# Where the chunked scan stands in the order of emission: each group's scan behind the next group's projections

## The chip, the cores and the metric

The kernel runs on one core of a Trainium2 chip. The metric is the device time of one execution in microseconds (us). Each time is the median of several executions; the profile is of one execution of the same program. The engines are TensorE (PE, matmuls), VectorE (DVE), ScalarE (ACT), GpSimd (POOL) and SyncE (SP), which issues most DMAs.

## The reference, cut to what matters

One layer of a hybrid backbone over 512 latent tokens and 256 context tokens, in float32. One input projection feeds three branches: a bidirectional chunked scan (SSD), a pooling mixer and a gated branch (gMLP). They are merged, projected and followed by a mixture of experts. The part in question:

```python
xbc = silu(dwconv(cols[..., :XBC_W], conv_w, conv_b))      # x, B, C of 4 groups, 5 taps
dt = softplus(cols[..., XBC_W:] + dt_bias)
# per direction, per group, chunks of 128:
acum = cumsum(dt * a)
decay = exp(where(tri, acum_i - acum_j, -inf))
y_diag = (C B^T * decay) @ (x * dt)
states = B^T @ (x * dt * exp(acum_last - acum))             # then a scan over the chunks
y_off = (C @ h_in) * exp(acum)
y = y_diag + y_off, both directions added; y_ssd = rmsnorm((y + d_skip * x) * silu(z))
# gated branch
u, v = gelu(uv); v = layernorm(v); y_gmlp = u * (ws @ v + bs)
# pooling branch: box means of width 2, 4, 8, 16 over the 8 x 64 grid, minus the input, then a matmul
```

## The kernel before

Every float32 weight comes by a DMA of 512 KB into a `raw` buffer (four), is split into a high part on ACT (L87, `hi`, three buffers) and a low part (L89, `lo`, three buffers), and goes into three matmuls: high by high, high by low, low by high. In the stage of the change POOL computes the low part (`lo_eng` is G).

Projections take one of three forms. `xbc_tile` (L997) projects 128 channels of x, B or C over 512 tokens (24 matmuls of 512 columns) and, but for C, over 256 context tokens (24 of 256), and hands the result to `conv_tile` (L951): copies on ACT into `xr` (two buffers), a first tap on ACT (L967), four taps on DVE (L969), silu on ACT, six transposes on PE (L989, L991) and copies to token order on ACT (L992, L993). `tm_block` (L1134) projects 512 columns in token order with 96 matmuls into all four accumulator banks (`pacc`); `z_block` (L1164) and `v_block` (L1210) use it. `cm_block` (L1148) projects 256 channels with 48 matmuls into two banks; pooling, `u_block` and the gates use it.

The scan works on four groups of four heads. For each group g:
- `bc(g)` and `xx(g)`: B and C, then two tiles of x, by `xbc_tile`;
- `ssd_decay(g)` (L1107): for four chunks, C B^T on PE (L1115), masks on DVE, the decay from a row that is broadcast by DMA from DRAM (`agb`, two buffers, L1111), exponentials on ACT, all joined in `w` (L1124 to L1132). `w` has four buffers, one group's worth;
- `z_block` for even g: the silu-gated z of two groups, into `ytok`;
- `ssd_group(g)` (L1053): the scan. DVE weights x (`xe`, L1061 to L1063), then five steps for two directions: a state matmul (L1074) and two DVE operations (L1083, L1084); then for each chunk matmuls with the states (L1093) and with `w` (L1095), and five DVE operations (L1099 to L1103), the last of which multiplies into `ytok`.

BT, CT, btok and xtok have two buffers each, so two groups can be held at once. Three PSUM banks (`ptmp`) serve the transposes, the products of the decay and the scan.

Behind the four groups the gated and the pooling branch are emitted as: pooling block 1, `v_block`, pooling block 0, `pool_out(1)`, `u_block(0)`, `pool_out(0)`, `u_block(1)`. Pooling is mostly DVE additions (L1259 to L1279) on `hx`, a tile that takes the buffer of the context tokens' `hC`; its matmul is on L1285. `v_block` writes its normalised v into `hx` too, and `u_block` mixes it (L1231). Then come the norm of the scan's output (squares on L1309), the gates and the merge.

The order on the engines' queues is not the order of emission. A framework lays out each engine's queue when the program is built: it goes by its own estimate of durations, and of the instructions that it takes to be ready the one that was emitted first goes first. On the chip each queue runs strictly in the order laid out. The order in which the Python code calls the steps is therefore a precedence. Before the change it is:

```python
for g in range(4):
    bc(g); xx(g); ssd_decay(g)
    if g % 2 == 0: z_block(g // 2)
    ...                                # g == 0: mix_prep(), params2(), zero
    nc.sync.dma_start(...)             # zero fill of one part of eod, from tile zero
    ssd_group(g)
```

Of the kernel before, what the change touches and what calls it, by code (L numbers as in the profile page):

```python
# [7 lines left out]
FT = mybir.dt.float32  # L8
# [3 lines left out]
AF = mybir.ActivationFunctionType  # L12
OP = mybir.AluOpType
# [16 lines left out]
OFF_GMLP = 3616  # L30
OFF_GATE = 4640
PW = 7712
# [6 lines left out]
def dap(t, off, ap):  # L39
    return bass.AP(tensor=t.tensor, offset=t.offset + off, ap=ap)  # L40
# [3 lines left out]
def backbone_kernel(ctx: ExitStack, tc: tile.TileContext, x, c, ctxt, c_ctx, w_mod, b_mod, g_norm1,  # L44
# [3 lines left out]
    nc = tc.nc  # L48
    V, S, G, T = nc.vector, nc.scalar, nc.gpsimd, nc.tensor
# [11 lines left out]
    eod = drp.tile([L, D], FT)  # L61
# [6 lines left out]
    small = ctx.enter_context(pool("small", 2))  # L68
# [679 lines left out]
    hcp = ctx.enter_context(pool("hcp"))  # L748
# [131 lines left out]
    zero = ssd.tile([128, 128], FT)  # L880
# [226 lines left out]
    def ssd_decay(g):  # L1107
        for cc in range(4):
            t = 2 + cc
            agb = ep.tile([128, 2, 4, 128], FT, tag="agb", name="agb")  # L1110
            nc.sync.dma_start(agb.rearrange("p d k i -> p (d k i)"),  # L1111
                              dap(agd, (cc * 4 + g) * 1024, [[0, 128], [1, 1024]]))
            cs = slice(cc * 128, (cc + 1) * 128)
            pcb = ptmp([128, 128])
            T.matmul(pcb, lhsT=BT[g][:, cs], rhs=CT[g][:, cs], start=True, stop=True)  # L1115
            cbl = ep.tile([128, 128], FT, tag="cbl", name="cbl")
            cbu = ep.tile([128, 128], FT, tag="cbu", name="cbu")
            V.tensor_tensor(cbl, pcb, mge, op=OP.mult)
            V.tensor_tensor(cbu, pcb, mle, op=OP.mult)
            w = epw.tile([128, 4, 128], FT, tag="w", name="w")  # L1120
            e = agb[:, 0]
            for k in range(4):
                f, b = g * 4 + k, 16 + g * 4 + k
                S.activation(w[:, k], agb[:, 1, k], AF.Identity, bias=nag[:, t, b:b + 1])  # L1124
                V.scalar_tensor_tensor(e[:, k], agb[:, 0, k], ag[:, t, f:f + 1], w[:, k],  # L1125
                                       op0=OP.subtract, op1=OP.min)
            S.activation(e, e, AF.Exp)
            for k in range(4):
                f, b = g * 4 + k, 16 + g * 4 + k
                S.activation(w[:, k], cbu, AF.Copy, scale=dtt[:, t, b:b + 1])  # L1130
                V.scalar_tensor_tensor(w[:, k], cbl, dtt[:, t, f:f + 1], w[:, k], op0=OP.mult, op1=OP.add)  # L1131
            wts[g, cc] = w, V.tensor_tensor(w, w, e, op=OP.mult)  # L1132
# [36 lines left out]
    def bc(g):  # L1169
        xbc_tile(8 + g)  # L1170
        xbc_tile(12 + g)

    def xx(g):
        xbc_tile(2 * g)
        xbc_tile(2 * g + 1)

    for g in range(4):
        bc(g)
        lo_eng[0] = G
        xx(g)  # L1180
        ssd_decay(g)
        if g % 2 == 0:
            z_block(g // 2)
        if g == 0:
            mix_prep()
            params2()
            with tc.issue_after(wts[0, 3][1].ins):
                V.memset(zero, 0.0)
        nc.sync.dma_start(dap(eod, g * 1024, [[4096, 128], [128, 8], [1, 128]]),
                          zero[:, None, :].to_broadcast([128, 8, 128]))  # L1190
        ssd_group(g)
    lo_eng[0] = G
    sq_.close()

# [7 lines left out]

    with ExitStack() as p3:
        gp = p3.enter_context(pool("gp"))
        hx = hcp.tile([128, 4096], FT, tag="h", name="hx")
        vt = hx[:, 0:2048].rearrange("p (t n) -> p t n", t=4)
        xps = [hx[:, n:n + 640].rearrange("p (r q) -> p r q", r=8) for n in (2048, 2688)]
        m = hx[:, 3328:3840].rearrange("p (t n) -> p t n", t=4)

        def v_block():  # L1210
            pv = tm_block(w_in, PW, OFF_GMLP + 512)
            for t in range(4):
                v = vt[:, t]
                S.activation(v, pv[t], AF.Gelu_apprx_tanh)
                bn = small.tile([128, 6], FT, tag="bn", name="bn")
                mv = small.tile([128, 2], FT, tag="mv", name="mv")
                rv = small.tile([128, 1], FT, tag="rv", name="rv")
                V.bn_stats(bn, v)
                V.bn_aggr(mv, bn)
                rsqrt(rv, mv[:, 1:2], 1.0, 1e-5, slice(0, 1))  # L1220
                V.tensor_scalar(v, v, mv[:, 0:1], rv, op0=OP.subtract, op1=OP.mult)

        def u_block(b):
            pu = cm_block(w_in, PW, OFF_GMLP + b * 256, hTh, hTl)
            for i in range(2):
                g = b * 2 + i
                u = gp.tile([128, 512], FT, tag="u", name="u", bufs=2)
                S.activation(u, pu[i], AF.Gelu_apprx_tanh)
                pmx = ptmp([128, 4, 128])
                for t in range(4):  # L1230
                    T.matmul(pmx[:, t], lhsT=vt[:, t, g * 128:(g + 1) * 128], rhs=wsT[:, g], start=True,  # L1231
                             stop=True)
                V.scalar_tensor_tensor(m, pmx, pcol[:, 68 + g:69 + g], mixb[:, g, None, :].to_broadcast([128, 4, 128]),
                                       op0=OP.mult, op1=OP.add)
                mf = m.rearrange("p a b -> p (a b)")
                V.tensor_tensor(mf, mf, u, op=OP.mult)
                split_to(ygh[:, g], ygl[:, g], mf)

        po_ = {}

        def pool_block(b, engs):
            pp = cm_block(w_in, PW, OFF_POOL + b * 256, hTh, hTl)
            for i in (1, 0):
                gi = b * 2 + i
                E = engs[i]
                w = WINDOWS[gi]
                h = w // 2
                xp_ = xps[i]
                G.memset(xp_[:, :, 0:8], 0.0)
                G.memset(xp_[:, :, 72:80], 0.0)  # L1250
                S.activation(xp_[:, :, 8:72], pp[i].rearrange("p (r q) -> p r q", r=8), AF.Copy)
                src, n = xp_, 80
                st = 1
                bufs = [gp.tile([128, 8, 80], FT, tag=f"b{j}", name=f"b{j}") for j in range(2)]
                nb = 0
                while st < w:
                    n -= st
                    d = bufs[nb % 2]
                    E.tensor_tensor(d[:, :, :n], src[:, :, :n], src[:, :, st:st + n], op=OP.add)  # L1259
                    src, nb, st = d, nb + 1, st * 2  # L1260
                rp = gp.tile([128, 24, 64], FT, tag="rp", name="rp")
                G.memset(rp[:, 0:8], 0.0)
                G.memset(rp[:, 16:24], 0.0)
                E.tensor_tensor(rp[:, 8:16], src[:, :, 8 - h:72 - h],
                                inv[:, gi, None, 0:64].to_broadcast([128, 8, 64]), op=OP.mult)
                src, r0, nr = rp, 8 - h, 7 + w
                st = 1
                rb = [gp.tile([128, 24, 64], FT, tag="r0", name="r0"), rp]
                nb = 0
                while st < w:  # L1270
                    nr -= st
                    d = rb[nb % 2]
                    E.tensor_tensor(d[:, :nr], src[:, r0:r0 + nr], src[:, r0 + st:r0 + st + nr], op=OP.add)
                    src, r0, nb, st = d, 0, nb + 1, st * 2
                o = gp.tile([128, 512], FT, tag=f"o", name=f"o", bufs=2)
                o3 = o.rearrange("p (r q) -> p r q", r=8)
                E.tensor_tensor(o3, src[:, 0:8], inv[:, gi, 64:72].unsqueeze(2).to_broadcast([128, 8, 64]),
                                op=OP.mult)
                E.tensor_tensor(o3, o3, xp_[:, :, 8:72], op=OP.subtract)  # L1279
                po_[gi] = o  # L1280

        def pool_out(b):
            for gi in (b * 2, b * 2 + 1):
                py = ptmp()
                T.matmul(py, lhsT=pwt[:, gi], rhs=po_[gi], start=True, stop=True)  # L1285
                S.activation(yph[:, gi], py, AF.Copy, scale=pcol[:, 64 + gi:65 + gi])
                V.scalar_tensor_tensor(ypl[:, gi], py, pcol[:, 64 + gi:65 + gi], yph[:, gi].bitcast(FT),
                                       op0=OP.mult, op1=OP.subtract)

        pool_block(1, (V, V))  # L1290
        v_block()
        pool_block(0, (V, V))
        pool_out(1)
        u_block(0)
        pool_out(0)
        u_block(1)
# [88 lines left out]
```

## Time and profile before

| | |
|---|---|
| median of 3 runs | 1046.08 us (1045.48 to 1047.08) |
| the profiled execution | 1043.95 us, of which 1042.2 us is the span of the profile |
| busy of the span | PE 954.0 us (92%), DVE 821.9 (79%), ACT 597.0 (57%), POOL 186.0 (18%) |
| chain of work that ended last | PE 64%, DVE 24%, ACT 6% |
| granted TensorE clock, mean | 0.977 of full speed |
| the four scans | the first state matmuls at about 136 us, the last product into `ytok` at 347.3 us |

A busy time is the time in which instructions of that engine ran, in us from the start of the span. A wait is idle time of an engine just before an instruction, put down to the instruction that released it. "DVE h L1084" is the instruction on line 1084 that writes tile h. A group on one line may hold several shapes.

### The profile page before, as it was taken

The numbers are of one execution on the slowest core, as the hardware profiler recorded it, in microseconds if no ns is written. First come the engines' busy times: TensorE is split into PE (matmuls) and PEld (weight loads), VectorE is DVE, ScalarE is ACT, GpSimd is POOL, SyncE is SP. The second block draws the span as 40 slices with busy tenths as digits, with TensorE's granted clock in tenths as the row PEclk, the third lists the DMA queues.
The fourth block names the chain that finished last, engine by engine and source line by source line (L and its number), as shares of the span: only waits on it lengthen the run. The fifth ranks groups of instructions, "written<-read, shape, count | busy, mean of one in ns | idle before, by whom it ended". The sixth has DMA issues, their size and how long they took to land.

```text
span 1042.2 us, 13348 instructions
## 1 busy us (share of the span) xinstructions
PE 954.0 (92%) x4598; PEld 767.3 (74%) x4598; DVE 821.9 (79%) x1221; ACT 597.0 (57%) x884; POOL 186.0 (18%) x144
## 2 busy tenths in 40 slices
PE   3898989998888979999999999969999999999964
PEld 0486778886777857878878788857888888888842
DVE  5877976997879995786476434579999999999897
ACT  5675846667465335532232332446787888888843
POOL 2033313213222330000000010330111111211140
PEclk9998999999999989999999999988999999999987
DMA  8922361314213212277476458578999999999212
GB/s 268 290 81 73 112 193 44 119 42 142 67 57 100 61 60 81 89 222 246 151 221 221 126 176 295 235 262 320 325 356 352 358 372 369 378 364 363 78 78 82
DMA packets 100897, 203.92 MB, mean 196 GB/s; under 512 B 9997, under 2 KB 55289, under 8 KB 100826
## 3 DMA queue, kind: packets, MB, share of 16 engines
q1 hardware_dynamic: 95474, 194.19, 53.6%
q0 software_dynamic: 5136, 8.78, 3.6%
q8 instruction: 37, 0.61, 0.2%
q14 instruction: 34, 0.28, 0.1%
q10 hardware_dynamic: 216, 0.07, 0.0%
HBM read 197.25 MB, written 13.71 MB: 202 GB/s over the span
## 4 chain that ended last, share of the span: by engine, by line
PE 64%; DVE 24%; ACT 6%; issue 4%; DMA 2%; POOL 0%; ACTq 0%; SPq 0%; DVEq 0%; POOLq 0%
PE pacc L104 18%; PE pacc L105 18%; PE pacc L103 18%; DVE cv L969 5%; DVE lo L89 2%; PE ptmp L399 1%; DVE w L1131 1%; PE ptmp L1093 1%; PE ptmp L1095 1%; DVE agb L1125 1%; ACT hi L87 1%; DVE w L1132 1%; DMA wraw<-in_w_mod_dram 1%; DVE xe L1061 1%; PE ptmp L422 1%
## 5 line engine op out<-in xcount | busy, mean ns | idle before, releaser
L87 ACT ACTIVATE hi<-raw 128x1024 fp32r<-128x1024 f32 (+1 forms) x199 | 209.2, 1057 | 175.8 <-PE pacc L104 81.7
L89 DVE TENSOR_TENSOR lo<-raw,hi 128x1024 fp32r<-128x1024 f32 (+1 forms) x165 | 204.1, 1255 | 61.3 <-ACT hi L87 54.8
L103 PE MATMUL pacc<-hTh,hi 128*128 128x512 f32 (+1 forms) x392 | 157.8, 403 | 4.9 <-ACT ytok L1167 3.1
L104 PE MATMUL pacc<-hTl,hi 128*128 128x512 f32 (+1 forms) x392 | 158.5, 405 | 0.0
L105 PE MATMUL pacc<-hTh,lo 128*128 128x512 f32 (+1 forms) x392 | 157.6, 403 | 0.0
L104 PE MATMUL pacc<-lo,xhl 128*128 128x512 f32 x384 | 152.9, 398 | 4.0 <-DVE lo L89 3.9
L103 PE MATMUL pacc<-hi,xhl 128*128 128x512 f32 x384 | 154.3, 405 | 0.0
L105 PE MATMUL pacc<-hi,xhl 128*128 128x512 f32 x384 | 152.2, 397 | 0.0
L89 POOL TENSOR_TENSOR lo<-raw,hi 128x1024 fp32r<-128x1024 f32 x34 | 88.0, 2593 | 199.6 <-ACT hi L87 168.7
L103 PEld LDWEIGHTS pacc<-hTh,hi 128*128 128x128 f32 (+1 forms) x392 | 73.4, 187 | 23.1 <-ACT ytok L1167 3.6
L104 PEld LDWEIGHTS pacc<-lo,xhl 128*128 128x128 f32 x384 | 73.2, 191 | 21.2 <-DVE lo L89 5.7
L969 DVE SCALAR_TENSOR_TENSOR cv<-xr,pcol,cv 128x770 f32<-128x770 f32 (+1 forms) x64 | 71.1, 1111 | 22.0 <-ACT cv L967 21.4
L105 PEld LDWEIGHTS pacc<-hTh,lo 128*128 128x128 f32 (+1 forms) x392 | 73.7, 188 | 17.6 <-issue 0.8
L104 PEld LDWEIGHTS pacc<-hTl,hi 128*128 128x128 f32 (+1 forms) x392 | 73.7, 188 | 17.4 <-issue 0.8
L105 PEld LDWEIGHTS pacc<-hi,xhl 128*128 128x128 f32 x384 | 72.7, 190 | 17.1 <-DVE xhl L401 0.3
L103 PEld LDWEIGHTS pacc<-hi,xhl 128*128 128x128 f32 x384 | 72.9, 190 | 15.5
L142 DVE SCALAR_TENSOR_TENSOR lacc<-raw,sc,lacc 128x1024 f32<-128x1024 f32 x32 | 41.1, 1283 | 28.5 <-DMA raw<-in_w_mod_dram 28.0
L89 DVE TENSOR_TENSOR lo<-r,hi 128x1024 fp32r<-128x1024 f32 x42 | 50.5, 1221 | 5.4 <-PE pacc L104 4.4
L87 ACT ACTIVATE hi<-r 128x1024 fp32r<-128x1024 f32 x42 | 44.1, 1061 | 8.7 <-PE pacc L105 6.9
L479 POOL DMA_INDIRECT xg<-h2d,toki x16 | 19.1, 1191 | 159.8 <-PE ptmp L399 73.8
L1144 PE MATMUL pacc<-lo,hTh 128*128 128x512 f32 x96 | 38.9, 406 | 0.0
L1143 PE MATMUL pacc<-hi,hTh 128*128 128x512 f32 x96 | 38.6, 402 | 0.0
(410 smaller groups left out, 1890.6 us busy)
## 6 DMA issues: line engine op xcount, KB each, us to landing
raw<-in_w_e_in_dram SPq DMA_DIRECT2D x78, 512.0 KB
raw<-in_w_in_dram SPq DMA_DIRECT2D x60, 512.0 KB
raw<-in_w_e_out_dram SPq DMA_DIRECT2D x36, 512.0 KB
raw<-in_w_mod_dram SPq DMA_DIRECT2D x32, 512.0 KB
r<-in_w_e_in_dram SPq DMA_DIRECT2D x28, 512.0 KB
wraw<-in_w_mod_dram SPq DMA_DIRECT2D x16, 512.0 KB
agb<-agd SPq DMA_DIRECT2D x16, 512.0 KB
r<-in_w_e_out_dram SPq DMA_DIRECT2D x14, 512.0 KB
```

The lines of the kernel that those rows point to most:

```text
L87: S.activation(hi[:, :n], raw[:, :n], AF.Copy)
L89: eng.tensor_tensor(lo[:, :n], raw[:, :n], hi[:, :n].bitcast(FT), op=OP.subtract)
L103: T.matmul(ps, lhsT=sh, rhs=mh, start=first, stop=False)
L104: T.matmul(ps, lhsT=sh, rhs=ml, start=False, stop=False)
L105: T.matmul(ps, lhsT=sl, rhs=mh, start=False, stop=last)
L142: V.scalar_tensor_tensor(a, raw, sc[:, k:k + 1], a, op0=OP.mult, op1=OP.add)
L399: T.transpose(pt[:, k], xgt[:, (h * 4 + k) * 128:(h * 4 + k + 1) * 128], ident)
L422: T.transpose(pt[:, k], hid[:, k * 128:(k + 1) * 128], ident)
L479: G.indirect_dma_start(out=dst, out_offset=None, in_=h2d[:, :], in_offset=bass.IndirectOffsetOnAxis(ap=idx, axis=0), bounds_check=L - 1, o ...
L969: V.scalar_tensor_tensor(oo, r[:, lo0 + j:lo0 + j + n], wcol(j), oo, op0=OP.mult, op1=OP.add)
L1143: T.matmul(pv[t], lhsT=a, rhs=wh[:, kk], start=k == 0, stop=False)
L1144: T.matmul(pv[t], lhsT=a, rhs=wl[:, kk], start=False, stop=False)
```

## The change

The call of `ssd_group` moves. For g = 1, 2, 3 the scan of group g-1 is emitted after `xx(g)` and ahead of `ssd_decay(g)`. The last scan, group 3, is emitted after the loop, behind `v_block`, which for this moves out of the gated branch and ahead of everything of it; the tile `hx` is allocated there as well. The zero fill becomes a function and is called where it stood. The functions' bodies are the same.

```diff
+    def zero_out(g):
+        nc.sync.dma_start(dap(eod, g * 1024, [[4096, 128], [128, 8], [1, 128]]),
+                          zero[:, None, :].to_broadcast([128, 8, 128]))
+
+    def v_block(hx):
+
+        vt = hx[:, 0:2048].rearrange("p (t n) -> p t n", t=4)
+        pv = tm_block(w_in, PW, OFF_GMLP + 512)
+        for t in range(4):
+            v = vt[:, t]
+            S.activation(v, pv[t], AF.Gelu_apprx_tanh)
...
+            V.tensor_scalar(v, v, mv[:, 0:1], rv, op0=OP.subtract, op1=OP.mult)
+        return vt
+
     for g in range(4):
         bc(g)
         lo_eng[0] = G
         xx(g)
+        if g:
+            ssd_group(g - 1)
         ssd_decay(g)
         if g % 2 == 0:
             z_block(g // 2)
...
-        nc.sync.dma_start(dap(eod, g * 1024, [[4096, 128], [128, 8], [1, 128]]),
-                          zero[:, None, :].to_broadcast([128, 8, 128]))
-        ssd_group(g)
+        zero_out(g)
+    hx = hcp.tile([128, 4096], FT, tag="h", name="hx")
+    vt = v_block(hx)
+    ssd_group(3)
     lo_eng[0] = G
     sq_.close()
...
-        hx = hcp.tile([128, 4096], FT, tag="h", name="hx")
-        vt = hx[:, 0:2048].rearrange("p (t n) -> p t n", t=4)
...
         pool_block(1, (V, V))
-        v_block()
         pool_block(0, (V, V))
         pool_out(1)
         u_block(0)
```

## Rows read from the trace of the kernel before

**Rows 1.** Busy time by stretch; columns: stretch, length, then engines.

```profile
core 0: us, PE busy (x) PEld busy (x) DVE busy (x) ACT busy (x) POOL busy (x), PEclk, DMA share, GB/s
127.00:389.50 262.50, 236.72 (x1216) 195.81 (x1214) 224.75 (x419) 146.43 (x273) 73.55 (x43) 0.99 0.29 89
158.00:389.50 231.50, 208.70 (x1070) 172.64 (x1068) 199.80 (x367) 130.00 (x241) 67.54 (x40) 0.99 0.25 78
264.00:286.00 22.00, 19.01 (x101) 16.15 (x100) 20.99 (x38) 9.01 (x18) 7.26 (x3) 1.00 0.21 63
314.00:389.50 75.50, 66.35 (x300) 52.51 (x299) 73.28 (x146) 32.26 (x60) 25.13 (x20) 0.95 0.23 71
405.00:640.00 235.00, 234.97 (x1044) 189.80 (x1044) 142.19 (x166) 83.08 (x113) 7.16 (x13) 1.00 0.56 180
```

**Rows 2.** Convolution groups of DVE, 158 to 187, then 264 to 286 us.

```profile
L969 DVE SCALAR_TENSOR_TENSOR cv<-xr,pcol,cv 128x770 f32<-128x770 f32 (+1 forms) x13 | 14.0, 1080 | 8.2 <-ACT cv L967 8.0
...
L969 DVE SCALAR_TENSOR_TENSOR cv<-xr,pcol,cv 128x770 f32<-128x770 f32 x4 | 4.0, 1012 | 0.0
```

**Rows 3.** PE in order of time: start us, us, line, what.

```profile
250.72 0.40 PE L1145 MATMUL pacc<-hi,hTl 128*128 128x512 f32 x1
250.95 1.46 PE L1074 MATMUL ptmp<-xe,btok 128*128 128x256 f32 x6
...
403.27 1.95 PE L1231 MATMUL ptmp<-wsT,hx 128*128 128x128 f32 x16
```

**Rows 4.** Waits of PE, 127 to 405 us: total, times, longest.

```profile
PE ptmp L1285 <- DVE o L1279: 6.8, 2, 5.5
PE ptmp L989 <- ACT cv L982: 6.3, 5, 2.6
PE ptmp L1074 <- DVE h L1084: 5.8, 4, 3.0
PE pacc L103 <- ACT ytok L1167: 3.1, 1, 3.1
PE ptmp L1095 <- DVE h L1084: 1.4, 1, 1.4
PE ptmp L1093 <- DVE h L1084: 1.3, 1, 1.3
```

**Rows 5.** DVE in order of time; in brackets the idle time before.

```profile
180.09 1.59 DVE L969 SCALAR_TENSOR_TENSOR cv<-xr,pcol,cv 128x770 f32<-128x770 f32 x1 [3.81 <-ACT cv L967]
...
240.66 3.73 DVE L1061 TENSOR_TENSOR xe<-xtok,dtde 128x1280 f32<-128x1280 f32 x1
...
282.81 2.14 DVE L1102 TENSOR_TENSOR y<-y,xd 128x256 f32<-128x256 f32 x1
...
305.21 1.59 DVE L969 SCALAR_TENSOR_TENSOR cv<-xr,pcol,cv 128x770 f32<-128x770 f32 x1 [3.81 <-ACT cv L967]
...
388.81 0.69 DVE L1279 TENSOR_TENSOR o<-o,hx 128x512 f32<-128x512 f32 x1
```

**Rows 6.** Zero fill on SP: count, min/median/max ns, first and last start.

```profile
L1189 SPq DMA_DIRECT2D eod<-zero x4: 366/574/1299, 134.1 to 140.4; - x4
```

**Rows 7.** Waits of DVE, 127 to 405 us.

```profile
DVE cv L969 <- ACT cv L967: 15.3, 6, 4.2
...
DVE xe L1062 <- ACT xtok L992: 5.6, 3, 2.0
```

**Rows 8.** POOL in order of time, three of its weight splits.

```profile
178.46 2.40 POOL L89 TENSOR_TENSOR lo<-raw,hi 128x1024 fp32r<-128x1024 f32 x1 [6.16 <-ACT hi L87]
...
282.28 2.38 POOL L89 TENSOR_TENSOR lo<-raw,hi 128x1024 fp32r<-128x1024 f32 x1 [11.10 <-ACT hi L87]
...
303.57 2.41 POOL L89 TENSOR_TENSOR lo<-raw,hi 128x1024 fp32r<-128x1024 f32 x1 [2.33 <-ACT hi L87]
```

**Rows 9.** Line 1102, all sixteen: min/median/max ns.

```profile
L1102 DVE TENSOR_TENSOR y<-y,xd x16: 410/418/2635, 150.9 to 346.8; 128x256 f32<-128x256 f32 x16
```

**Rows 10.** Waits of ACT, 127 to 405 us.

```profile
ACT w L1124 <- PE ptmp L1095: 20.2, 6, 6.7
```

**Rows 11.** Line 1309, first and last start.

```profile
L1309 ACT ACTIVATE sqy<-ytok x4: 1044/1048/1057, 410.5 to 417.0; 128x1024 f32<-128x1024 f32 x4
```

More of the change, by code (lines that the diff above doesn't have):

```diff
@@ L1175, in xx @@
         xbc_tile(2 * g + 1)
+    def zero_out(g):
[7 more added lines that the diff above has]
+            S.activation(v, pv[t], AF.Gelu_apprx_tanh)
+            bn = small.tile([128, 6], FT, tag="bn", name="bn")
+            mv = small.tile([128, 2], FT, tag="mv", name="mv")
+            rv = small.tile([128, 1], FT, tag="rv", name="rv")
+            V.bn_stats(bn, v)
+            V.bn_aggr(mv, bn)
+            rsqrt(rv, mv[:, 1:2], 1.0, 1e-5, slice(0, 1))
+            V.tensor_scalar(v, v, mv[:, 0:1], rv, op0=OP.subtract, op1=OP.mult)
+        return vt
     for g in range(4):
@@ L1204, in backbone_kernel @@
         gp = p3.enter_context(pool("gp"))
-        hx = hcp.tile([128, 4096], FT, tag="h", name="hx")
-        vt = hx[:, 0:2048].rearrange("p (t n) -> p t n", t=4)
         xps = [hx[:, n:n + 640].rearrange("p (r q) -> p r q", r=8) for n in (2048, 2688)]
         m = hx[:, 3328:3840].rearrange("p (t n) -> p t n", t=4)
[L1210 to L1221, printed above, removed]
         def u_block(b):
```

## The prediction

> **What bounds the kernel now.** I read the page first: TensorE (PE) has the largest busy share of the span, VectorE (DVE) the next. Shares over the whole span say little, so I cut out the stage of the change, from the first z block's end (127 us) to the last `u_block`'s mixing matmuls (403.27 us [rows 3]), and looked at it by stretches [rows 1]. The reader is to see two engines that are both nearly full: from 127 to 389.5 PE is busy 236.7 of 262.5 us, DVE 224.8. They take turns at being late. Under the second group's projections DVE has 14.0 us of convolution and sits 8.2 us waiting for it [rows 2]; from 314 to 389.5, last decay, last scan and pooling, DVE is busy 73.3 of 75.5 us, and PE waits. Behind 405 PE runs without a gap (234.97 of 235 us), so what is won or lost before that point passes on one for one, and 403.27 is my marker.
>
> Third, the waits of PE [rows 4]. The six largest add to 24.7 us. The scan's own chain (state matmul, two DVE operations, next state matmul) accounts for 8.5 (5.8 + 1.4 + 1.3), transposes waiting for a convolution for 6.3, the pooling matmul for 6.8, and 3.1 is the z block's evacuation. If none of them were left, the marker would stand at 403.3 - 24.7 = 378.6: no order of emission gains more than about 25 us while PE's work stays.
>
> Fourth, the order on PE's queue, which says what emission order means here. At 240.66 + 3.73 = 244.4 us the inputs of the third group's state matmuls are ready [rows 5], yet the z block, emitted earlier, runs on to 250.95 and only then do they come [rows 3]. So of what is ready the earlier emitted goes first, and the later is starved. The change works through this alone.
>
> **The change part by part.** No arithmetic is removed or added; PE's, DVE's, ACT's and POOL's work is the same.
>
> *The zero fill of the output buffer.* Its four DMAs go at 134 to 140 us, all of them, three of them far ahead of where they are emitted [rows 6]. They need only the zero tile. Cost 0; weight loads stand behind them on SP as now.
>
> *Scans 0 to 2 behind the next projections.* Now scan g goes ahead of group g+1's projections and fills DVE during the first of them. After the change PE serves the four projection tiles first, and the scan's matmuls wait until PE has nothing else ready. DVE then has only convolution under the projections, and scan and decay together behind them. This does not fill DVE's idle time under the projections; it moves it forward by one scan and leaves more work ready behind each block of projections. I count DVE's work from 158 us, about where scan 0 ends now: 199.8 us of work and 31.7 of idle time up to 389.5 [rows 1]. Scan 0 comes into it: from 264 to 286 us DVE is busy 20.99, of which 4.0 is convolution [rows 1, 2], so a scan is 17.0 us. About half of the second group's convolution (14.0 us) goes out of it, being done earlier: -7.0. Sum 209.8 us.
>
> Of the 31.7 us of idle time, convolutions waiting for their first pass on ACT and `xe` waiting for `xtok` are 15.3 + 5.6 = 20.9 [rows 7]. In these places a deferred scan is now at hand. Bounds: none of it is recovered (the scan's matmuls are starved exactly then) or all of it. I take half, 10.4, since the waits lie in the middle and at the end of a block of projections, and only those at the end find the scan released. Idle left 21.3 us.
>
> *Collisions with POOL.* POOL splits the weights (`lo`, 2.4 us each). Two of the splits, at 178.46 and 303.57 us [rows 8], fall where DVE waits 3.8 us for a convolution; one at 282.28 falls on a scan, and there the addition on L1102 takes 2.14 us [rows 5], where its median is 0.418 and its worst 2.635 [rows 9]. With DVE full, a split that cost nothing costs up to 2.635 - 0.418 = 2.2 us: 0 to 4.4 us for these two, and I take the upper end, because some others reach an idle DVE in part. The Trainium skill ("SBUF — State Buffer", Who interferes with whom) says that a DVE instruction with two SBUF inputs contends with a GpSimd instruction that reads SBUF, and that one of them blocks for the whole instruction. That speaks against packing DVE work tighter beside POOL, and the trace agrees (0.418 against 2.14 us).
>
> *The w buffers.* There are four, one group's worth, and decay g+1 writes them after scan g has read them. ACT waits 20.2 us for that already [rows 10]. After the change decay g stands right behind scan g-1, which is itself late. Cover: PE has the z block or the next projections to run meanwhile. No cost on PE as long as these are left; where they are used up, it is the chain of the slow case below.
>
> *The v block ahead of the last scan.* Its 96 matmuls (22 us at 0.23 us from one to the next [rows 3]) are filler in the last scan now. They come forward, to the place where pooling block 1 is projected now. Their four DMAs and splits go ahead of two others on SP and POOL, with the same total. Its DVE work is small and stays before the end of pooling. Its evacuation may be held up by ACT as the z block's is: 0 to 3.1 us [rows 4], taken at 0 because pooling's projections follow. In exchange the last scan and pooling have pooling's and both `u_block`s' matmuls as cover. What this acts on is PE's 6.8 us wait for pooling [rows 4] and the 13.8 us from the last pooling operation (ends 389.5 [rows 5]) to the marker, of which `u_block(1)`'s 48 matmuls are 48 x 0.23 = 11.2. They can run under the pooling, which leaves 2.6 us behind it.
>
> *The last scan later.* Its output is read first by the squares on L1309 at 410.5 us [rows 11], while DVE goes over to pooling some 60 us earlier. Cost 0; the cover would be gone only if the scan slipped past 400.
>
> **Sum.** DVE's end of pooling: 158 + 209.8 + 4.4 + 21.3 = 393.5 us (389.5 now). Marker: 393.5 + 2.6 = 396.1 against 403.3, a gain of 7.2 us, with 17.5 of PE's 24.7 us of waits left. On the profiled execution of 1043.95 us (1042.2 span and 1.75 around it) that is 1036.8; the median of the runs shown, 1046.08, is 2.1 above that execution, so the forecast is 1039 us.
>
> **The rivals.** *Filled completely:* all 20.9 us of idle time are recovered and no new collisions come. 158 + 209.8 + 10.8 + 2.6 = 381.2, a gain of 22 us: 1024 us. For it: the waits are of the kind that other ready work fills. Against it: strict precedence of projections [rows 3], and PE's floor of 378.6 is only 3 us away.
>
> *Backlog, slower than before:* the scan is starved through the projections, nothing of the idle time is recovered, and a whole extra scan (17 us of DVE) stands behind the last projections in one chain: scan 2, decay 3 (which needs its w buffers), scan 3, pooling. A scan with nothing beside it has idle time of its own: from 264 to 286 it takes 22 us for 17 of work, and convolution fills the rest, which the last scan no longer has. With one such 5 us: 158 + 209.8 + 4.4 + 31.7 + 5 + 2.6 = 411.5, 8.2 us late: 1054 us; with two, 1059. It decides when idle time and collisions behind 158 us exceed 403.3 - 2.6 - 158 - 209.8 = 32.9 us. For it: DVE is already full from 314 to 389.5. Against it: `u_block(1)`'s 11.2 us of PE work come out of the tail.
>
> *The waits trade places:* the pooling wait goes, and waits for w buffers or the v block's evacuation come. 1046 us, within 2.
>
> **How the numbers follow.** A measurement of this kernel can tell about 0.2% (2.1 us) from no change. Forecast (2 to 15 us faster) 0.47, filled completely 0.15, trade 0.14, backlog 0.24. Faster 0.62, same 0.14, slower 0.24. The range goes from near the filled case to the first price of the backlog: 1026 to 1054. As cases of both signs hold much of the chance, the forecast's own range is 1031 to 1044.
>
> **What would show it.** Right: state matmuls of scan g-1 behind the last projection of group g; PE's wait for pooling (6.8 us) gone or short; `u_block(1)`'s matmuls ahead of the last pooling matmul; DVE's end of pooling within 388 to 397. Wrong: DVE idle by more than 33 us between 158 and the end of pooling; waits of PE for h, or of ACT for w, over 30 us together; more than 3 us between the v block's last matmul and its evacuation with PE idle.

## The result: slower by 2.4%

The changed kernel takes 1071.84 us (median of 6 runs, 1070.46 to 1072.52) against 1045.87 us before. The ratio is 1.0239, with a 95% interval of 1.0221 to 1.0256. The forecast was 1039 us in a range of 1026 to 1054: wrong in sign, and the measured time lies outside the range. The backlog rival had the sign right and the size wrong (1054 to 1059).

The profiled execution has a span of 1069.3 us at a mean granted clock of 0.957 (1042.2 us at 0.977 before). The first fence is the busy time by stretch in the changed kernel; the columns are those of [rows 1].

```profile
core 0: us, PE busy (x) PEld busy (x) DVE busy (x) ACT busy (x) POOL busy (x), PEclk, DMA share, GB/s
127.00:158.00 31.00, 28.01 (x138) 23.11 (x138) 14.33 (x26) 20.89 (x36) 8.77 (x4) 0.94 0.64 182
158.00:417.30 259.30, 221.50 (x1081) 182.54 (x1080) 209.75 (x397) 129.64 (x242) 63.72 (x39) 0.91 0.23 67
127.00:429.20 302.20, 261.41 (x1265) 214.65 (x1265) 230.90 (x431) 154.72 (x283) 72.49 (x42) 0.92 0.27 80
431.00:666.00 235.00, 234.99 (x1044) 189.67 (x1043) 142.09 (x166) 83.10 (x113) 7.17 (x13) 1.00 0.58 180
```

One row of the kernel before, of the same view, up to its marker, stands beside the third of these:

```profile
127.00:403.30 276.30, 250.02 (x1269) 205.64 (x1268) 232.53 (x428) 150.63 (x280) 73.55 (x43) 0.99 0.29 88
```

The marker moved from 403.27 to 429.20 us, 25.9 us later. Behind it PE is busy 234.99 of 235 us as before, so the delay passes on: 25.9 of the 27.1 us by which the span is longer. The 25.9 us have two parts. PE's idle time up to the marker went from 276.3 - 250.0 = 26.3 to 302.2 - 261.4 = 40.8 us: +14.5. PE's busy time for the same matmuls (1269 and 1265 records) went from 250.0 to 261.4 us: +11.4, with the granted clock at 0.92 instead of 0.99.

PE in order of time in the changed kernel (start, duration, line; in brackets the wait before it) shows the places on which the rest turns. L1240 and L1294 are L1231 and L1285 of before.

```profile
174.76 0.44 PE L989 MATMUL ptmp<-ident,cv 128*128 128x128 f32 x2 [0.94 <-ACT cv L982]
175.03 0.60 PE L991 MATMUL ptmp<-ident,cv 128*128 128x128 f32 x4
175.47 1.76 PE L1074 MATMUL ptmp<-xe,btok 128*128 128x256 f32 x7
...
339.17 0.39 PE L1145 MATMUL pacc<-hi,hTl 128*128 128x512 f32 x1
339.40 1.46 PE L1074 MATMUL ptmp<-xe,btok 128*128 128x256 f32 x6
...
354.32 3.78 PE L1074 MATMUL ptmp<-xe,btok 128*128 128x256 f32 x8 [7.89 <-ACT hc L1076]
361.07 1.22 PE L1074 MATMUL ptmp<-xe,btok 128*128 128x256 f32 x2 [2.96 <-DVE h L1084]
...
408.77 3.78 PE L1294 MATMUL ptmp<-o,pwt 128*128 128x512 f32 x4 [8.12 <-DVE o L1288]
...
419.11 1.88 PE L1294 MATMUL ptmp<-o,pwt 128*128 128x512 f32 x4
...
429.20 1.95 PE L1240 MATMUL ptmp<-wsT,hx 128*128 128x128 f32 x16
```

The reader is to see three things. Scan 0 starts at 175.47 us (136.5 before), right behind the last transposes of the next group's convolutions; scans 1 and 2 do the same at 240.53 and 312.07. The last scan starts at 339.40, right behind the v block's last projection matmul, and from 346.4 PE stands still for 7.9 us. And the second `u_block`'s matmuls are partly behind the pooling's matmul of 419.11, not under the pooling.

Waits of PE from 127 to 431 us (total, times, longest), to be held against [rows 4]:

```profile
PE ptmp L989 <- ACT cv L978: 8.8, 3, 4.3
PE ptmp L1294 <- DVE o L1288: 8.1, 1, 8.1
PE ptmp L1074 <- ACT hc L1076: 7.9, 1, 7.9
PE ptmp L989 <- ACT cv L982: 6.6, 6, 2.7
PE ptmp L1074 <- DVE h L1084: 4.2, 2, 3.0
PE pacc L103 <- ACT ytok L1167: 4.1, 2, 2.4
```

Transposes that wait for a convolution take 15.4 us (6.3 before), the pooling's matmul 8.1 (6.8), and the last scan's first step 7.9 (not there before). Waits of DVE from 158 us to the end of pooling at 417.3:

```profile
DVE cv L969 <- ACT cv L967: 25.8, 6, 5.2
DVE h L1083 <- ACT hc L1076: 8.2, 3, 2.7
DVE y L1099 <- PE ptmp L1093: 4.8, 5, 3.6
DVE w L1131 <- ACT w L1130: 4.6, 5, 1.7
DVE y L1101 <- PE ptmp L1095: 3.2, 5, 0.7
```

The wait for the convolution's first pass, which the deferred scans were to fill, rose from 15.3 [rows 7] to 25.8 us. Only the 5.6 us of `xe` went.

### The profile page after: what moved, and what is told of

The parts are those of the page before. It is cut to its first block, busy times and chain, and to the rows that moved or that the text cites. A ratio compares the mean times of both kernels' runs of the same rounds, so it can differ in the third digit from the quotient of the medians.

```text
span 1069.3 us, 13345 instructions
## 1 busy us (share of the span) xinstructions
PE 966.3 (90%) x4598; PEld 777.0 (73%) x4598; DVE 820.1 (77%) x1221; ACT 599.2 (56%) x885; POOL 186.3 (17%) x144
## 4 chain that ended last, share of the span: by engine, by line
PE 66%; DVE 19%; ACT 8%; issue 4%; DMA 2%; POOL 0%; ACTq 0%; DVEq 0%; SPq 0%; POOLq 0%
PE pacc L103 17%; PE pacc L104 17%; PE pacc L105 17%; DVE cv L969 5%; DVE lo L89 2%; PE ptmp L399 1%; PE ptmp L1074 1%; ACT hi L87 1%; DVE agb L1125 1%; ACT w L1130 1%; PE ptmp L1093 1%; DVE b L1268 1%; PE ptmp L1095 1%; ACT L1127 1%; PE ptmp L422 1%
## 5 line engine op out<-in xcount | busy, mean ns | idle before, releaser
L969 DVE SCALAR_TENSOR_TENSOR cv<-xr,pcol,cv 128x770 f32<-128x770 f32 (+1 forms) x64 | 76.6, 1204 | 37.1 <-ACT cv L967 36.1
L103 PEld LDWEIGHTS pacc<-hi,xhl 128*128 128x128 f32 x384 | 73.2, 191 | 15.6
```

Source lines behind the costliest of these rows:

```text
L103: T.matmul(ps, lhsT=sh, rhs=mh, start=first, stop=False)
L969: V.scalar_tensor_tensor(oo, r[:, lo0 + j:lo0 + j + n], wcol(j), oo, op0=OP.mult, op1=OP.add)
```

## Experiments: the two halves

The start of the last decay (first L1115 of group 3) divides the loss: 313.7 us before, 326.7 after (+13.0); from there to the marker 89.6 before, 102.5 after (+12.9). Two kernels took one half each; the diffs of this and the next two sections are against the changed kernel, unless another is named.

The loop alone:

```
         if g:
             ssd_group(g - 1)
         ssd_decay(g)
...
-    hx = hcp.tile([128, 4096], FT, tag="h", name="hx")
-    vt = v_block(hx)
     ssd_group(3)
+    hx = hcp.tile([128, 4096], FT, tag="h", name="hx")
...
         pool_block(1, (V, V))
+        vt = v_block(hx)
         pool_block(0, (V, V))
```

> Only the first half of the change: scans 0 to 2 stand behind the next group's projections and convolutions, the last scan and everything behind it as in the kernel before. In the changed kernel the last group's decay (L1115) starts 13 us later than before (326.7 against 313.7 us), and from there to the marker (the start of the second u block's mixing matmuls) it takes 102.5 us against 89.6, so the loss has two halves of 13 us. Two-halves theory: +13 us, 1059 us (1055 to 1063), last L1115 at about 327. Rival, the loop's delay is swallowed by the waits of the tail and all loss is in the tail: 1046 (within 3). Rival, the loop alone is the whole of it, because a late scan drags the tail: 1070 (over 1066).

Measured: 1057.94 us, ratio 1.0115 (1.0082 to 1.0148), so +11.9 us; the last decay starts at 329.3. For the loop the two-halves theory holds. From 127 us to that point, this kernel first and the one before second:

```profile
127.00:329.30 202.30, 179.31 (x918) 150.87 (x919) 146.43 (x263) 112.57 (x212) 46.70 (x23) 0.96 0.30 88
```

```profile
127.00:313.70 186.70, 170.07 (x916) 143.00 (x915) 151.35 (x273) 113.92 (x213) 48.42 (x23) 1.00 0.31 95
```

Of the 15.6 us that the loop is longer, 9.2 are PE busy longer on the same matmuls (clock 0.96 against 1.00), 6.4 are PE idle.

The tail alone:

```
-        if g:
-            ssd_group(g - 1)
         ssd_decay(g)
...
         zero_out(g)
+        if g < 3:
+            ssd_group(g)
     vt = v_block(hx)
     ssd_group(3)
```

> Only the second half of the change: the loop as in the kernel before, the last scan behind the gated branch's v block. Two-halves theory: the last decay starts at about 314 us as before, the v block's evacuation and the last scan, with nothing of DVE's beside it, take 13 us more: 1059 us (1055 to 1063). Rival, the tail was slow in the changed kernel only because the third scan reached into it: 1046 (within 3). My recorded forecast for this part alone: about 5 us faster, since the second u block's matmuls lie under the pooling.

Measured: 1051.21 us, ratio 1.0046 (1.0029 to 1.0064), +5.1 us; the last decay starts at 316.4, the marker is at 413.1. Slower, so my forecast of 5 us faster for this part fell; the size is well under half of the 13 that the two-halves theory gave, so for the tail that theory fell too. The halves add to 17.0 us, and the whole change costs 25.8 by the same kind of comparison: 8.8 us come only when both are there.

## Experiments: what holds the late scans back

My step called Fourth said that of what is ready the earlier emitted goes first, and that the change works through this alone. The changed kernel's order suggests another holder. The scan's state tiles, the transposes of the convolutions and the products that the masks read share three PSUM banks. If a bank is handed out in order of emission, a tile that is emitted behind a group's transposes waits until these have had their banks. The row of before on which the step rests (L1074 at 250.95 [rows 3]) fits both, since the masks read the last two of the decay's products until 250.1 and 250.5 us. So precedence and place of emission were taken apart.

The place kept late, the old precedence given back to scans 0 to 2:

```
+        p0 = tc.tile_snap_priority()
         bc(g)
         lo_eng[0] = G
         xx(g)
+        prio[g] = tc.tile_snap_priority() - p0
         if g:
-            ssd_group(g - 1)
+            with tc.high_priority(prio[g]):
+                ssd_group(g - 1)
```

> The changed kernel with the place of emission kept, but scans 0 to 2 given the precedence that they had before (their priority is that of the place ahead of group g's projections). Buffers are still handed out in order of emission. Precedence theory, which the prediction used (its Fourth): the state matmuls run as early as in the kernel before, the loop's 13 us are gone, the tail's stay: about 1059 (1054 to 1063). PSUM-ring theory: precedence changes nothing, since the tile of the first state matmul waits for the banks of the last transposes: first L1074 of scan 0 at 175 us as in the changed kernel, time 1072 (1067 to 1076).

Measured: 1064.26 us, ratio 1.0164 (1.0128 to 1.0201), between the two numbers. The place of the scan decides the reading. PE in order of time in this kernel:

```profile
178.77 0.44 PE L989 MATMUL ptmp<-ident,cv 128*128 128x128 f32 x2 [0.94 <-ACT cv L982]
179.05 0.27 PE L991 MATMUL ptmp<-ident,cv 128*128 128x128 f32 x1
179.16 1.01 PE L1074 MATMUL ptmp<-xe,btok 128*128 128x256 f32 x3
```

With all its precedence the scan still stands behind the last transposes, and the last decay starts at 326.3 us as in the changed kernel (326.7). So in the loop precedence alone gives nothing back; what this kernel gains lies in the tail (96.7 us from the last decay to the marker, against 102.5).

The scan emitted half as far back, between a group's B and C blocks and its x blocks (the last scan and the v block stand as in the kernel before, which the diff leaves out):

```
         bc(g)
         lo_eng[0] = G
+        if g:
+            ssd_group(g - 1)
         xx(g)
-        if g:
-            ssd_group(g - 1)
```

> Scan g-1 emitted half as far back: behind group g's B and C blocks, ahead of its x blocks, so that its PSUM tiles are asked for ahead of the transposes of the x blocks; the last scan as in the kernel before. PSUM-ring theory (the state tiles share three PSUM banks with the convolutions' transposes and get them in order of emission): the state matmuls now come under the x blocks' projections, DVE has them as work there, and most of the loop's loss is gone: 1040 to 1052. Precedence theory (what is emitted later is starved as long as an earlier matmul is ready): the state matmuls come only when PE has nothing else, before the x blocks as long as these are emitted later, so it gives about the same place; the two differ in the next run, not in this one. Rival, any move of the scan behind a projection costs the same: 1056 to 1062.

Measured: 1058.72 us, ratio 1.0120 (1.0082 to 1.0158): my 1040 to 1052 was wrong, the rival (any such move costs the same) came out. The first state matmul is at 150.42 us, again right behind the last transposes emitted ahead of it (149.99). Its last decay starts at 323.7, 10.0 us later than before; by the same windows as above PE is busy 176.71 us for 918 matmuls there, 6.6 more than before, at a clock of 0.96. Half the way back brings no time back: this kernel costs 12.6 us and the loop alone 11.9, though its scan 0 starts 29 us earlier than there. Why it costs as much was not tested.

A first split of the banks gave the state tiles a bank of their own and left two for all else. It is read against the same split of the kernel before.

```
-    tmp = ctx.enter_context(pool("tmp", 3, PSUM))
+    tmp = ctx.enter_context(pool("tmp", 2, PSUM))
+    stp = ctx.enter_context(pool("stp", 1, PSUM))
...
-                st = ptmp([128, 4, 64])
+                st = stp.tile([128, 4, 64], FT, tag="st", name="st")
```

> Control for the two runs that follow: the kernel before, with the three shared PSUM banks split into two shared ones and one of its own for the scan's state tiles. Its price is that of one shared bank fewer: 1046 if the transposes and masks never need three, up to 1060 if they do. The two runs that follow are read against it.

> The changed kernel with the same split: the state tiles no longer wait for the banks of the convolutions' transposes, the place of emission and with it the precedence stay late. Read against the split kernel before; the change without the split costs 25.8 us. PSUM-ring theory alone: the state matmuls run as soon as their inputs are there, the loop's 12 us are gone, the tail's stay: 5 to 14 us over the control. Precedence alone: no difference, 22 to 30 over the control. Both together (either is enough to hold the scan back): a little earlier at best, 18 to 28 over the control.

> The changed kernel with the split and with the old precedence for scans 0 to 2: neither the banks nor the precedence hold the scan back, only the place of emission is late. Giving back the precedence alone took 7.6 of the 25.8 us away. If the two are together the whole of the loop's loss, the state matmuls of scan 0 run under the next group's first projections as in the kernel before (first L1074 about 137 to 145 us) and what is left is the tail's part: 5 to 14 us over the control. Rival, the loop loses for another reason (the slower clock and the waits for the convolutions come whatever the scan does): 17 to 26 over the control.

Measured: control 1055.24 us (1.0093 of the kernel before); the whole change on the split 1061.06, 5.8 us over the control; with the old precedence besides 1063.59, 8.3 over. The first lies in the 5 to 14 that I had named for the banks as the only holder, and outside what I had named for precedence alone (22 to 30) and for either one being enough (18 to 28); the second lies in the 5 to 14 for both lifted. But the old precedence makes the time no shorter here, so the times don't rank the two, and the scan's other tiles (`pfb`, `pd2`) still come from the shared banks. The place of the scan says more. PE in order of time, with the precedence given back:

```profile
126.12 0.60 PE L1075 MATMUL st<-xe,btok 128*128 128x256 f32 x2
...
140.18 0.59 PE L1075 MATMUL st<-xe,btok 128*128 128x256 f32 x2
...
182.66 0.60 PE L992 MATMUL ptmp<-ident,cv 128*128 128x128 f32 x4
183.30 0.92 PE L1094 MATMUL ptmp<-h,CT 128*128 128x256 f32 x3
```

The state matmuls, with a bank of their own, start at 126.12 us and go on from 140.18 under the next projections, as in the control (127.07 and 140.23). The output matmuls of the same scan (L1094), with the same precedence but in the shared banks, come 43 us later, right behind the last transposes. With the late precedence, in the whole change on this split:

```profile
174.19 0.28 PE L106 MATMUL pc<-hC,lo 128*128 128x256 f32 x1
174.31 0.59 PE L1075 MATMUL st<-xe,btok 128*128 128x256 f32 x2
```

Here the same tiles, in the same bank of their own, wait for the next group's last projection: precedence alone holds them too. That this kernel still costs only 5.8 us over its control is a matter of the tail: from the last decay to the marker it takes 89.8 us, the control 91.8, and the changed kernel without the split 102.5. The 7.9 us wait of the last scan is not there. So the tail's part of the loss needs the shared banks as well; how they make it was not tested.

A cleaner split gives the transposes the bank of their own and leaves the whole scan in the other two.

```
-    tmp = ctx.enter_context(pool("tmp", 3, PSUM))
+    tmp = ctx.enter_context(pool("tmp", 2, PSUM))
+    trp = ctx.enter_context(pool("trp", 1, PSUM))
...
-        p1_, p2_ = ptmp(), ptmp()
+        p1_, p2_ = [trp.tile([128, 512], FT, tag="tr", name="tr") for _ in range(2)]
```

It was run in the kernel before (control), with the late loop alone, with the late loop and the old precedence, and with the whole change.

> Control for the three runs that follow: the kernel before with the convolutions' transposes in a PSUM bank of their own and two shared banks for all the rest, the whole scan among it. Its own price: 1044 to 1056 (the control with a bank for the state tiles alone cost 9).

> The first half of the change (scans 0 to 2 late, last scan and tail as before) on that split: the scan's tiles no longer wait for the transposes' banks, the precedence is late. The half cost 11.9 us with shared banks. If the shared banks alone held the scan: 0 to 3 us over the control. If precedence alone suffices to hold it: 9 to 15 over the control, first L1074 of scan 0 behind the last projections of group 1 (about 165 to 175 us).

> The same with the old precedence given back to scans 0 to 2: neither banks nor precedence hold them, the place of emission alone is late. If the two together are all that the loop lost: within 3 us of the control, first L1074 of scan 0 at 135 to 142 us. Rival, the place of emission acts through something else yet (the order of DVE's and ACT's queues, the single buffers of xe, xd and h): over 6 us above the control.

> The whole change on that split. If the shared banks carry a part of the loss: 8 to 20 us over the control, against 25.8 without the split. If precedence carries all of it: 23 to 29 over the control.

Measured: control 1056.07 us (ratio 1.0111, 1.0054 to 1.0167); late loop 1064.17, 8.1 over the control; late loop with the old precedence 1058.77, 2.7 over; whole change 1066.53, 10.5 over. One of the four control executions took 1064.3, so differences to the control are less sure than that between the two late loops, whose executions don't overlap. PE in order of time, late loop on the split:

```profile
168.95 0.29 PE L106 MATMUL pc<-hC,lo 128*128 128x256 f32 x1
169.07 1.03 PE L1075 MATMUL ptmp<-xe,btok 128*128 128x256 f32 x4
...
178.62 0.44 PE L990 MATMUL tr<-ident,cv 128*128 128x128 f32 x2
```

and with the old precedence:

```profile
140.09 0.59 PE L1075 MATMUL ptmp<-xe,btok 128*128 128x256 f32 x2
```

So the four cases stand like this (start of scan 0, 136.5 us before, 139.25 in the control):

| | shared banks | transposes apart |
|---|---|---|
| late precedence | 175.5 / 179.2 us (whole change / loop alone), loop alone +11.9 us | 169.1 us, +8.1 us over control |
| old precedence | 179.2 us, behind the last transposes (with the change's tail; the loop alone was not run) | 140.1 us, +2.7 us over control |

Either one holds the scan back, precedence by 30 us and the banks by 43; with both lifted the late place of emission costs 2.7 us, within the 3 that I had named and within the scatter of these runs. For the late loop on the split the expectation for banks alone (0 to 3) fell: precedence suffices to hold the scan, at the place that I had named (165 to 175 us). Its 8.1 us lie below the 9 to 15 that went with it. The whole change on the split lies in the 8 to 20 for the banks carrying a part. It costs 2.4 us more than the late loop on the same split, against 13.9 (25.8 - 11.9) with shared banks, which again puts much of the tail's loss on the shared banks. The control itself loses 10 us to the split, so these prices can't simply be added. The wait of DVE for the convolution's first pass follows the scan: 26.2 us with the late loop, 10.7 with both lifted, 11.7 in the control (127 to 400 us).

## Experiments: the tail

The tail alone, with the last scan's old precedence given back, so that the v block fills behind it (the diff is against the kernel of the tail alone):

```
+    p0 = tc.tile_snap_priority()
     vt = v_block(hx)
-    ssd_group(3)
+    with tc.high_priority(tc.tile_snap_priority() - p0):
+        ssd_group(3)
```

> The second half of the change alone (the loop as before, the last scan behind the v block), with the last scan's old precedence given back: it goes ahead of the v block's 96 matmuls, and the v block fills behind it. With the precedence late it cost 5.1 us: from the last decay's start to the last scan's end 49.6 us against 31.6 before, of which the pooling that follows (38.9 against 44.2) and the shorter way from pooling to the marker (8.2 against 13.8) give back 11. Theory, precedence starves the last scan: first L1074 of scan 3 comes right behind its inputs, 317 to 320 us, and with the 18 us gone and the two gains of up to 5 us kept the time is 1036 to 1046. Rival, the v block's evacuation (ACT's table loads and the square roots) holds the last scan up wherever it stands: 1049 to 1054.

Measured: 1045.87 us, ratio 0.9998 (0.9978 to 1.0017). PE in order of time, first without and then with the precedence:

```profile
331.65 0.39 PE L1145 MATMUL pacc<-hi,hTl 128*128 128x512 f32 x1
331.88 1.46 PE L1074 MATMUL ptmp<-xe,btok 128*128 128x256 f32 x6
```

```profile
317.46 0.59 PE L1074 MATMUL ptmp<-xe,btok 128*128 128x256 f32 x2
317.71 0.58 PE L1143 MATMUL pacc<-hi,hTh 128*128 128x512 f32 x1
```

The last scan starts 14.4 us earlier, its way from the last decay to its last matmul is 33.7 us (49.6 without, 31.6 before), and the 5.1 us are gone. In the tail it is precedence that starves the scan, by the v block's 96 matmuls. The gain that I had hoped for beyond that is not there: pooling ends at 393.8 us (389.5 before), and the marker is 11.7 us behind that. That pooling's projections now stand behind the v block's fits this, but was not tested.

The same in the whole change:

> The whole change, with only the last scan's precedence given back (ahead of the v block's 96 matmuls). The loop alone cost 11.9 us, the tail alone 5.1, the two together 25.8: 8.8 more than their sum. Theory, the surplus is the last scan starved behind the v block while the third scan, itself late, still uses DVE: with the last scan's precedence back, both the 5.1 and the 8.8 go and the loop's part is left: 1058 (1054 to 1062). Rival, the surplus belongs to the late third scan in whatever tail: 1063 to 1068.

Measured: 1063.51 us, ratio 1.0155 (1.0126 to 1.0184), 7.9 us less than the changed kernel and some 6 more than the loop alone. The rival's number came out: the precedence of the last scan is one part of the surplus, and a v block ahead of pooling costs more when the third scan is late. Why those 6 us remain was not tested further.

The remaining question was whether the one thing that I wanted from the tail, the `u_block`s' matmuls under the pooling, is worth anything by itself. In the kernel before:

```
-        pool_out(1)
         u_block(0)
+        pool_out(1)
         pool_out(0)
         u_block(1)
```

> The kernel before with one exchange: the first u block is emitted ahead of pooling's first output block. PE waits 6.8 us for pooling's results in the kernel before, 5.5 of it once at 372 us, with the first u block's matmuls queued behind the waiting matmul. If these waits are time on the path: 1040 to 1044. Rival, DVE (73.4 of 75.8 us busy from the last decay to the end of pooling) sets the end, and what PE does earlier only waits later: 1046 (within 2).

```
-        pool_out(1)
         u_block(0)
-        pool_out(0)
         u_block(1)
+        pool_out(1)
+        pool_out(0)
```

> The same with both u blocks ahead of both of pooling's output blocks: what the change's tail wanted, all of the u blocks' PE work under the pooling, without moving a scan or the v block. If PE's waits are on the path: 1036 to 1042. Rival, DVE sets the end: the second u block's DVE operations now stand ahead of pooling's last, and the time is 1046 (within 3).

Measured: 1044.95 us, ratio 0.9987 (0.9971 to 1.0003), and 1044.89, ratio 0.9991 (0.9976 to 1.0006): not to be told from no change. The waits of PE from 127 to 405 us with the first `u_block` ahead say why:

```profile
PE ptmp L1231 <- DVE hx L1221: 6.3, 1, 6.3
```

The 6.8 us wait for the pooling's result is gone, and the mixing matmul waits 6.3 us for the normalised v instead, which stands behind the pooling on DVE. So DVE's work sets the end of this stage here, and PE's wait only changes its name. None of these kernels beats the one before.

## Why the prediction was wrong, step by step

**What held.** The marker passes on one for one. DVE's work behind 158 us was put at 209.8 + 4.4 = 214.2 us and measured 209.75. The `w` buffers cost PE nothing: ACT's wait for them is 21.6 us against 20.2 [rows 10]. The zero fill left no trace in any wait. And the point from which the backlog decides was right: idle time and collisions over 32.9 us; DVE was idle 259.30 - 209.75 = 49.6. Of the three signs of being wrong this one came, and so did the one of the v block's evacuation: its last gelu starts at 353.40 us, 13.8 behind the v block's last matmul, and PE is idle from 346.4 on. The third stayed under its mark (PE for `h` 4.2 and ACT for `w` 21.6 us, 25.8 together, against 30).

**The sum, term by term.** The forecast put the end of pooling at 393.5 and the marker at 396.1 us; measured 417.3 and 429.2, 33.1 us later. Idle time of DVE: 21.3 forecast, 49.6 measured, +28.3. DVE's work with collisions: -4.5. From the end of pooling to the marker: 2.6 forecast, 11.9 measured, +9.3. Together 33.1.

**The failed step: "In these places a deferred scan is now at hand."** I recovered half of 20.9 us of idle time, which leaves 10.5. Measured are 25.8 us in these places, 15.3 more, and with the 11.5 of the lone scans (below) that is nearly all of the 28.3. No scan came to hand, as shown by scan 0 at 175.47. That DVE loses a scan's work from 127 to 158 us (busy 14.3 us there, 25.0 before) was in the sum; that nothing fills the places behind was not. The precedence rule in Fourth already said that a scan emitted behind the projections is starved as long as these are ready; I used it to say that the scan comes late and then counted on it in the middle of the projections all the same. And the rule was half of the mechanism: the shared banks, which I hadn't read out of the code (`st`, `pfb`, `pd2`, `p1_`, `p2_` and `pcb` all come from the same three), hold the scan behind the last transposes even with its precedence restored. That either holds the scan is shown by the runs, and for precedence its price too (8.1 us on the split against 2.7 without it); the price of the banks alone was not measured.

**The term that wasn't in the sum: the clock.** 11.4 us of the marker's delay are PE being busy longer on the same matmuls. I had counted PE's waits as idle time only. The section on the hardware has the rows.

**The lone scan.** In the backlog case I gave 5 us of idle time to each scan that has nothing beside it, in the forecast none. DVE's waits inside the scans (`h`, and the two on `y`) went from 4.7 to 16.2 us, +11.5: right in kind, twice the size of one. The POOL collision came too, at another place than I named: in the last scan three splits run back to back on POOL (7.32 us from 355.56), and two multiplications of DVE on L1083 take 4.59 us together and the next 2.12 (0.415 is the median of one), while PE waits for the result.

**The v block forward and the last scan later, both taken at 0.** The tail alone cost 5.1 us, and its cure by precedence shows the place: the last scan starts behind the v block's matmuls. The v block's evacuation was priced as a wait of PE for PSUM (0 to 3.1 us). What it did in the changed kernel lies on ACT, in order of time:

```profile
346.16 1.28 ACT L110 ACT_TABLE_LOAD   x1
347.46 0.20 ACT L110 ACTIVATE rs<-rs 128x1 f32<-128x1 f32 x1
347.68 1.28 ACT L1127 ACT_TABLE_LOAD   x1
...
350.50 1.28 ACT L110 ACT_TABLE_LOAD   x1
...
352.10 1.28 ACT L1187 ACT_TABLE_LOAD   x1
...
353.89 0.65 ACT L1076 ACTIVATE hc<-ptmp 128x256 f32<-128x256 f32 x2
```

From 337.5 to 353.9 us ACT alternates between gelu, the decay's exponential and the square roots, six table loads of 1.28 us among them, and the scan's first copy (L1076), for which PE has been waiting since 346.4, comes last. From the last decay to the marker ACT makes nine loads here and four in the kernel before. The tail alone with the old precedence makes four as well, so it can't tell what the loads cost. The whole change with the old precedence for the last scan makes eight, and PE never waits for `hc` in it: this wait needs the scan behind the loads. That the loads alone made the 7.9 us was not tested.

**The second `u_block` under the pooling (2.6 us left behind).** The matmuls of pooling's first output block wait 8.1 us at 408.77, and what is queued behind them on PE waits too: 36 of the second `u_block`'s 48 projection matmuls come after 419.11. 11.9 us are left. (48 x 0.23 is 11.0, not the 11.2 of my sum; the slip is worth 0.2 us.) The two exchanges of `u_block`s show that in the kernel before the time doesn't fall without this wait either.

## What to carry to other kernels

Before a stage is moved back in the order of emission, list what it shares with the work that it is moved behind: precedence on the queue, and every ring of buffers that both draw from. Late in either was late in fact here; idle time that lies under the work moved ahead was then not filled by what was moved behind it. And price a new wait of PE twice: once as idle time, and once as the slower matmuls that may follow it (14.5 and 11.4 us here).

## What the hardware showed that I had not expected

PE's waits cost more here than their own length. The granted clock by stretch in the changed kernel, around the 7.9 us wait:

```profile
338.00:346.00 8.00, 8.00 (x36) 6.60 (x35) 6.33 (x22) 7.96 (x19) 0.00 (x0) 1.00 0.32 118
346.00:354.00 8.00, 0.43 (x2) 0.00 (x0) 6.28 (x28) 7.88 (x14) 0.00 (x0) 0.67 0.00 1
354.00:366.00 12.00, 7.45 (x16) 4.97 (x17) 11.94 (x24) 4.87 (x7) 7.32 (x3) 0.50 0.48 130
366.00:378.00 12.00, 12.00 (x62) 10.31 (x61) 7.59 (x20) 0.60 (x1) 0.00 (x0) 0.87 0.00 1
378.00:400.00 22.00, 22.00 (x99) 17.98 (x99) 19.77 (x19) 3.67 (x4) 10.55 (x11) 1.00 0.24 72
```

PE stands still from 346.4 to 354.3. In the next 12 us, in which it works with further waits between, the clock is 0.50 throughout, the lower of its two levels (1.2 GHz against 2.4). It rises within the stretch from 366, in which PE has no wait (mean 0.87), and is at full speed from 378. At the lower level a pair of state matmuls took 1.22 us (361.07) where a pair took 0.59 at full speed (317.46 in the run of the tail). Up to the marker PE's busy time is 11.4 us longer for the same matmuls, nearly as much as the added idle time of 14.5. Most of it does not come from this place, though, but from the loop. From 127 us to the last decay, to be held against the row of before in the first section of experiments:

```profile
127.00:326.70 199.70, 179.14 (x919) 150.52 (x919) 144.43 (x263) 111.67 (x210) 46.96 (x22) 0.96 0.30 89
```

That is 9.1 us more at a clock of 0.96 instead of 1.00; 2.3 us come behind it.

A switch of ACT's table costs little more than 1.28 us here: the square root's load at 346.16 begins 0.01 us after the copy before it ends (345.76 + 0.39), and the square root follows at 347.46. The Trainium skill ("ScalarE: Activation LUTs", What ACT_TABLE_LOAD costs) gives about 1.28 us for the load, which agrees, and about 1.38 us of draining on top of it, 2.66 in all, which these rows don't show.
